# Two transformer blocks on one core: output gates computed inside the mLSTM heads, convolution taps run into the merge

## The chip, the cores and the metric

The kernel runs on one core of a Trainium2 chip. The metric is the device time of one execution in microseconds (us); the median of three runs of the kernel before is 3096.0 us (3094.24 to 3097.0). Five engines work beside each other: TensorE (PE) does the matrix products and transposes, VectorE (DVE), ScalarE (ACT) and GpSimd (POOL) the elementwise work, and SyncE (SP) issues the loads of weights.

## The reference, cut to what matters

Two depth-2 networks run one after the other over 256 tokens of width 1024 (the first has 256 context tokens beside them in its layer 0). The change touches only the first network's mixers: attention, a bidirectional mLSTM with four heads, and a convolution of 31 taps, merged by three sigmoid gates.

```python
def mlstm_readout(h, o_pre, norm_w, w_o):
    b, _, n, _ = h.shape
    hn = rmsnorm(h.transpose(0, 2, 1, 3), norm_w.reshape(MLSTM_HEADS, MLSTM_HEAD_DIM)).reshape(b, n, MLSTM_DIM)
    return (hn.astype(o_pre.dtype) * jax.nn.sigmoid(o_pre)) @ w_o

def conformer_conv(u, dw_w, dw_b, ln_w, ln_b, w_o):
    a, g = jnp.split(u, 2, axis=-1)
    h = dwconv(a * jax.nn.sigmoid(g), dw_w, dw_b)
    return jax.nn.silu(layernorm(h, ln_w, ln_b)) @ w_o
...
    def merge(conv_o, mlstm_o, attn_o, gate_pre):
        g_conv, g_mlstm, g_attn = jnp.split(jax.nn.sigmoid(gate_pre + branch_gate_b), N_BRANCH, axis=-1)
        return (g_conv * conv_o + g_mlstm * mlstm_o + g_attn * attn_o) @ w_out
```

## The kernel before, in words

Every large product is done in three passes (L414 to L416): weights and activations are split into a high and a low part, and high*high, high*low and low*high are added in PSUM. A chunk of eight 128x128 weight blocks is loaded by SP (L344), split by ACT and DVE into `wh` and `wl` (L323, L307), and taken in a fixed order from a stream (`_Stream.take`). `lin` multiplies one 128-wide strip of weights with all tokens: 24 products when the depth is eight blocks. Layer 0 of the first network works on 512 tokens (`nq` = 512), layer 1 on 256.

`mixers` (L784) goes through one layer's token mixers. First come the mLSTM's gate rows, the keys, values and queries of attention; then, by the list `ORDER` (L61), alternating heads ("m") and quarters of the convolution ("c"): m0 c0 m1 c1 m2 c2 m3 c3. A head (`mlstm`, L1136) computes q and k, the score tiles S (L1217) and the values V (L1171, the lines L435 to L437), and queues one follow-up per token segment (`mlstm_seg`, L1231; two segments in layer 0, one in layer 1). A follow-up is a chain: a row spread on PE (L1267), exponentials and products on DVE and ACT that make the weight tiles `mEh` and `mEl`, the products with V (L1309 to L1311), this twice (once for each direction), then the norm (POOL, L1251), four transposes (L1257) and a copy into `hs` (L1259). A quarter of the convolution (`glu_conv`, L1071) is two `lin`s and then 31 taps on DVE (L1097). After the last quarter come the output gates: eight `lin`s of `mlstm_gate` (L1195), whose tanh is multiplied into `hs` by a follow-up named "ogate".

Follow-ups lie in queues ("attn", "mlstm", "conv", "ogate") and are Python generators. Each `lin` credits all queues with its nominal time (`tick`, L393: 24 products of 512 columns count 5.12 us), and when the credit of a queue reaches its interval, one step of its generators is emitted. `flush` emits what is left. Steps marked `soon` get a higher priority, and a scheduler that runs when the kernel is built makes the final static order of each engine from priorities and simulated times. On the chip each engine follows that order and waits where a semaphore says so.

All tiles of the heads and of attention live in one memory pool, `head` (L795), which is closed after the flush of "mlstm", "ogate" and "attn" (L825). Then the pool `merge` is opened (L829) with the split inputs `bh` and `bl` and the sum `merged`. The merge takes attention's branch (`wba`), the convolution's (`wbc`, after `flush("conv")`) and the mLSTM's (`wbm`). For each 128 (layer 1: 256) output columns it does `po` (products with `bh` and `bl`, 4 or 8 blocks deep) and the gate's `pg` (products with the layer's own input, eight blocks deep), then tanh on ACT, a multiply on DVE and an add on POOL.

Of the kernel before, what the change touches and what calls it, by code (L numbers as in the profile page):

```python
# [24 lines left out]
AF = mybir.ActivationFunctionType  # L25
OP = mybir.AluOpType
# [5 lines left out]
KD = D // P  # L32
# [4 lines left out]
MH = 4  # L37
# [23 lines left out]
ORDER = [(kind, h) for h in range(MH) for kind in "mc"]  # L61
# [110 lines left out]
def _layout(inp):  # L172
# [11 lines left out]
    for l in range(DEPTH):  # L184
        w = a["w_in"][l]
# [7 lines left out]
        for kind, h in ORDER:  # L193
            if kind == "m":
                c = slice(h * 256, (h + 1) * 256)
                parts += [qkv[:, :1024][:, c], qkv[:, 1024:2048][:, c]]
            else:
                parts += [cu[:, h * P:(h + 1) * P], cu[:, 512 + h * P:512 + (h + 1) * P]]
        parts.append(mo)
# [15 lines left out]
        g = a["mlstm_gate_b"][l]  # L215
# [73 lines left out]
class _K:  # L289
# [494 lines left out]
    def mixers(self, l, st, xs, segs, nq):  # L784
# [5 lines left out]
        with ExitStack() as es:  # L790
# [4 lines left out]
            with tc.tile_pool(name=f"head{l}", bufs=1) as hp:  # L795
# [17 lines left out]
                for j in range(4):  # L813
                    for seg in segs:
                        self.queue("attn", (15.9 if l == 0 else 15) * slow, 2 if l == 0 else 1, self.attention(j, seg, seg * len(segs) // 2, kT, va, hp, ao))
                for kind, h in ORDER:
                    if kind == "m":
                        self.mlstm(l, h, st, xs, xq, segs, nq, rows, hp, hs)
                    else:
                        self.queue("conv", (6.4 if l == 0 else 8.7) * slow, 1,  # L820
                                   self.glu_conv(l, h, st, xq, segs, nq, mp, cv), early=False)
                self.queue("conv", (6.4 if l == 0 else 8.7) * slow, 1, self.conv_norm(l, nq, cv))
                for n in range(0, KD, G):
                    self.mlstm_gate(l, n, st, xq, nq, hs)
                for name in ("mlstm", "ogate", "attn"):  # L825
                    self.flush(name)
                if l == 0:
                    self.load_x()
            with tc.tile_pool(name=f"merge{l}", bufs=1) as gp:  # L829
                merged = gp.tile([P, KD, nq], F32, name="merged")  # L830
                for name, src, kt, b, first in (("wba", ao, 4, 2, True), ("wbc", cv, 4, 0, False),
                                                ("wbm", hs, 8, 1, False)):
# [303 lines left out]
    def mlstm(self, l, h, st, xs, xq, segs, nq, rows, hp, hs):  # L1136
# [26 lines left out]
        with self.soon():  # L1163
            S = [self.mlstm_scores(seg, i * 256, qT, kT, hp) for i, seg in enumerate(segs)]
        nc.gpsimd.tensor_copy(v[0][:, :, 256:258], self.onec[:, None, :].to_broadcast([P, 4, 2]))
# [13 lines left out]
        for i, seg in enumerate(segs):  # L1179
            self.queue("mlstm", (6.8 if l == 0 else 5.8), 2, self.mlstm_seg(h, seg, i * 256, nq, S[i], v, rows, hp, hs))  # L1180

# [13 lines left out]
    def mlstm_gate(self, l, n, st, xq, nq, hs):  # L1195

        G = 512 // nq
        bank = self.mmt()
        for i in range(G):
            self.lin(bank[:, i * nq:(i + 1) * nq], st["wi"], xq, KD)  # L1200
        t = self.tmp()
        with self.soon():
            self.act(t, bank, AF.Tanh, scale=0.5)
            for i in range(G):
                w = self.mnwh[l][:, n + i:n + i + 1]
                self.act(t[:, i * nq:(i + 1) * nq], t[:, i * nq:(i + 1) * nq], AF.Identity, scale=w, bias=w)

        def finish():
            if n // 2 == 3:
                self.flush("mlstm")  # L1210
            m = hs[:, n:n + G, :].rearrange("p g n -> p (g n)")
            self.tt(m, m, t, OP.mult)
            yield

        self.queue("ogate", (5.2 if l == 0 else 6.9), 1, finish())
# [15 lines left out]
    def mlstm_seg(self, h, seg, c0, nq, S, v, rows, hp, hs):  # L1231
# [27 lines left out]
        nc.scalar.copy(hs[:, 2 * h:2 * h + 2, c0:c0 + 256], pt.rearrange("p (e q) -> p e q", e=2))  # L1259
# [461 lines left out]
```

## Time and profile before

| what | value |
|---|---|
| median of three runs | 3096.0 us |
| profiled execution | 3097.4 us, of it a span of 3095.7 us |
| PE busy | 3047.0 us, 98% of the span, 21412 products |
| PE weight loads | 2745.8 us, 89% |
| DVE, ACT, POOL busy | 1866.6, 1468.1, 405.5 us |
| mean granted clock of TensorE | 0.994 |
| mixers and merge of layer 0 | about 44 to 690 us of the span |
| mixers and merge of layer 1 | about 1130 to 1548 us |

The profile gives, for each engine, when it was busy and what ended each wait. A matrix product shows as about 0.28 us (256 columns) because products overlap in the pipeline; what one costs is the distance from its start to the next one's. The granted clock is a share of 2.4 GHz, so 0.50 is 1.2 GHz. Times below are counted from the span's start.

### The profile page before, as it was taken

What the parts mean: (1) busy time and instruction counts of PE and PEld (TensorE: products, weight loads), DVE (VectorE), ACT (ScalarE), POOL (GpSimd) and SP (SyncE); (2) the same over time, 40 slices, a digit from 0 to 9 for tenths busy, and PEclk for the clock granted to TensorE, in tenths of its full rate; (3) what the DMA queues carried; (4) which work ended last, traced back from release to release, by engine and by line L of the source; (5) the groups of instructions that cost most, each with busy time, mean ns of one, the idle gap of its engine ahead of it and who ended that gap; (6) DMA issues with size and microseconds to landing.
All of it is one profiled execution on the core that took longest, in us unless ns stands there. A gap on an engine that the chain in (4) does not pass through costs nothing.

```text
span 3095.7 us, 52954 instructions
## 1 busy us (share of the span) xinstructions
PE 3047.0 (98%) x21412; PEld 2745.8 (89%) x21412; DVE 1866.6 (60%) x3064; ACT 1468.1 (47%) x2414; POOL 405.5 (13%) x419
## 2 busy tenths in 40 slices
PE   6999999999999999999999999999999999999999
PEld 4777878887777778899999999999999999999999
DVE  4467864336535546776587565576665665676664
ACT  4344463324323335455465444655544544654543
POOL 3212130112000033211100100122000000121000
PEclk9999999999999999999999999999999999999999
DMA  7423212324444423225555555444455554444553
GB/s 247 145 93 127 78 68 96 109 96 144 156 141 145 150 89 104 76 93 175 184 187 180 184 185 184 143 149 151 161 193 185 169 185 162 150 153 157 171 184 116
DMA packets 163429, 453.98 MB, mean 147 GB/s; under 512 B 14832, under 2 KB 66288, under 8 KB 162672
## 3 DMA queue, kind: packets, MB, share of 16 engines
q1 hardware_dynamic: 162464, 449.11, 43.9%
q8 instruction: 168, 2.75, 0.4%
q10 hardware_dynamic: 720, 1.49, 0.1%
q14 instruction: 77, 0.63, 0.1%
HBM read 447.13 MB, written 1.05 MB: 145 GB/s over the span
## 4 chain that ended last, share of the span: by engine, by line
PE 96%; DMA 1%; DVE 1%; ACT 1%; SPq 0%; issue 0%; POOL 0%; DVEq 0%; ACTq 0%; POOLq 0%
PE mm L414 25%; PE mm L416 25%; PE mm L415 25%; PE mm L436 2%; PE aux L605 2%; PE mm L437 2%; PE mm L435 2%; PE mm L428 1%; PE mm L429 1%; PE mm L427 1%; PE aux L1068 1%; DMA araw<-in_ada_dram 1%; PE aux L369 1%; PE aux L1569 1%; PE aux L1053 1%; PE aux L1043 1%
## 5 line engine op out<-in xcount | busy, mean ns | idle before, releaser
L307 DVE TENSOR_TENSOR wl<-raw,wh 128x1024 fp32r<-128x1024 f32 x746 | 922.2, 1239 | 780.9 <-ACT wh L323 763.0
L323 ACT CAST wh<-raw 128x1024 fp32r<-128x1024 f32 x746 | 782.5, 1051 | 1074.1 <-PE mm L415 736.4
L414 PE MATMUL mm<-xh,wh 128*128 128x256 f32 (+1 forms) x3680 | 1144.3, 311 | 4.2 <-ACT ao L301 3.0
L415 PE MATMUL mm<-xl,wh 128*128 128x256 f32 (+1 forms) x3680 | 1143.4, 311 | 0.0
L416 PE MATMUL mm<-xh,wl 128*128 128x256 f32 (+1 forms) x3680 | 1142.8, 311 | 0.0
L414 PEld LDWEIGHTS mm<-xh,wh 128*128 128x128 f32 x3680 | 699.3, 190 | 47.4 <-issue 8.4
L415 PEld LDWEIGHTS mm<-xl,wh 128*128 128x128 f32 x3680 | 699.5, 190 | 43.1 <-issue 9.6
L416 PEld LDWEIGHTS mm<-xh,wl 128*128 128x128 f32 x3680 | 699.3, 190 | 42.5 <-issue 7.5
L416 PE MATMUL mm<-ah,wl 128*128 128x256 f32 (+1 forms) x1056 | 317.5, 301 | 0.2 <-DVE wl L307 0.2
L415 PE MATMUL mm<-al,wh 128*128 128x256 f32 (+1 forms) x1056 | 317.6, 301 | 0.0
L414 PE MATMUL mm<-ah,wh 128*128 128x256 f32 (+1 forms) x1056 | 316.9, 301 | 0.0
L415 PEld LDWEIGHTS mm<-al,wh 128*128 128x128 f32 x1056 | 200.9, 190 | 9.1 <-issue 2.5
L416 PEld LDWEIGHTS mm<-ah,wl 128*128 128x128 f32 x1056 | 200.9, 190 | 9.1 <-issue 2.1
L414 PEld LDWEIGHTS mm<-ah,wh 128*128 128x128 f32 x1056 | 200.6, 190 | 8.7 <-issue 2.1
L310 POOL TENSOR_TENSOR small<-small,mhalf 128x2 f32<-128x2 f32 (+2 forms) x48 | 50.6, 1054 | 1051.7 <-DVE small L304 713.2
L310 POOL TENSOR_TENSOR ss<-ss,t 128x256 f32<-128x256 f32 (+1 forms) x68 | 72.1, 1061 | 623.7 <-ACT t L301 602.3
L304 DVE SCALAR_TENSOR_TENSOR cv<-glu,p,cv 128x512 f32<-128x512 f32 (+1 forms) x240 | 150.7, 628 | 3.5
L414 PE MATMUL mm<-bh,wh 128*128 128x512 f32 (+1 forms) x384 | 129.0, 337 | 1.3 <-ACT wh L323 0.7
L416 PE MATMUL mm<-bh,wl 128*128 128x512 f32 (+1 forms) x384 | 129.0, 337 | 0.3 <-DVE wl L307 0.3
L415 PE MATMUL mm<-bl,wh 128*128 128x512 f32 (+1 forms) x384 | 129.2, 337 | 0.0
L436 PE MATMUL mm<-wh,xl 128*128 128x256 f32 x448 | 127.8, 287 | 0.0
L437 PE MATMUL mm<-wl,xh 128*128 128x256 f32 x448 | 127.4, 286 | 0.0
(331 smaller groups left out, 4283.8 us busy)
## 6 DMA issues: line engine op xcount, KB each, us to landing
araw<-in_ada_dram SPq DMA_DIRECT2D x96, 512.0 KB, 3.9
raw<-in_a_wup_dram SPq DMA_DIRECT2D x88, 512.0 KB, 3.4
raw<-in_b_f1u_dram SPq DMA_DIRECT2D x88, 512.0 KB, 3.4
raw<-in_b_f2u_dram SPq DMA_DIRECT2D x88, 512.0 KB, 3.4
raw<-in_a_wi_dram SPq DMA_DIRECT2D x78, 512.0 KB, 3.3
raw<-in_b_wb_dram SPq DMA_DIRECT2D x72, 512.0 KB, 3.3
raw<-in_b_wi_dram SPq DMA_DIRECT2D x48, 512.0 KB, 3.4
raw<-in_a_wdn_dram SPq DMA_DIRECT2D x44, 512.0 KB, 3.3
```

Source lines behind the costliest of these rows:

```text
L304: self.nc.vector.scalar_tensor_tensor(out, in0, s, in1, op0=op0, op1=op1)
L307: self.nc.vector.tensor_tensor(out, in0, in1, op=op)
L310: self.nc.gpsimd.tensor_tensor(out, in0, in1, op=op)
L323: self.nc.scalar.copy(h, src)
L369: self.last_mm = self.nc.tensor.matmul(ps[0:32], x, x[:, 0:1].to_broadcast([P, 256]), start=True, stop=True).ins
L414: mm(ps, h, xh[:, k, cols], start=k == 0, stop=False)
L415: mm(ps, h, xl[:, k, cols], start=False, stop=False)
L416: self.last_mm = mm(ps, l, xh[:, k, cols], start=False, stop=k == kt - 1).ins
L435: mm(ps, xh, w[0], start=start, stop=False)
L436: mm(ps, xl, w[0], start=False, stop=False)
L437: mm(ps, xh, w[1], start=False, stop=stop)
L605: nc.tensor.matmul(ps[32 * j:32 * j + 32, c * 256:(c + 1) * 256], self.cpad[:, k, :], raw[:, j, :], start=k + c == 0, stop=k + c == KD)
```

## The change

The output gates move from the end of the heads into them: `mlstm_gate` runs for each head, before V in heads 0 to 2 and after V in head 3, and writes its tanh straight into `hs`. The follow-up's last step then multiplies the transposed result into `hs` (DVE) where it was copied before (ACT), and the queue "ogate" is gone. `ORDER` becomes one list for each layer: layer 0 is m0 c0 m1 c1 m2 m3 c2 c3, layer 1 stays m0 c0 m1 c1 m2 c2 m3 c3. Before c2 and c3 are computed, the "conv" queue is stepped until at most one earlier quarter is left. The intervals change: attention from 15.9 to 11.4 (layer 0) and from 9.0 to 7.5 (layer 1), the convolution from 6.4 to 8.0 (layer 0) and from 5.2 to 4.8 (layer 1). The merge takes the mLSTM's branch second and the convolution's last, so `flush("conv")` stands before the third branch.

```diff
@@ -58,7 +58,9 @@
 
 
 
-ORDER = [(kind, h) for h in range(MH) for kind in "mc"]
+
+ORDER = [[("m", 0), ("c", 0), ("m", 1), ("c", 1), ("m", 2), ("m", 3), ("c", 2), ("c", 3)],
+         [("m", 0), ("c", 0), ("m", 1), ("c", 1), ("m", 2), ("c", 2), ("m", 3), ("c", 3)]]
 
 STREAMS1 = {
     "wi": _chunks(WI_ORDER * KD),
@@ -190,13 +192,12 @@
         gates[:, 32:36], gates[:, 96:100] = mg[:, 8:12], mg[:, 12:16]
         rows = (np.arange(0, 512, 64)[:, None] + HALVES[None]).reshape(-1)
         parts = [gates, ak[:, rows[:P]], av, aq[:, rows][:, head]]
-        for kind, h in ORDER:
+        for kind, h in ORDER[l]:
             if kind == "m":
                 c = slice(h * 256, (h + 1) * 256)
-                parts += [qkv[:, :1024][:, c], qkv[:, 1024:2048][:, c]]
+                parts += [qkv[:, :1024][:, c], qkv[:, 1024:2048][:, c], mo[:, c]]
             else:
                 parts += [cu[:, h * P:(h + 1) * P], cu[:, 512 + h * P:512 + (h + 1) * P]]
-        parts.append(mo)
         s1["wi"].append(_pack(_fan(_blocks(np.concatenate(parts, axis=1)), 2), STREAMS1["wi"]))
         v = qkv[:, 2048:].reshape(2, KD // 2, P, MH, 256).transpose(3, 0, 2, 1, 4)
         s1["wv"].append(v.reshape(-1))
@@ -812,24 +813,25 @@
                     kT = self.key_parts(kT, hp)
                 for j in range(4):
                     for seg in segs:
-                        self.queue("attn", (15.9 if l == 0 else 15) * slow, 2 if l == 0 else 1, self.attention(j, seg, seg * len(segs) // 2, kT, va, hp, ao))
-                for kind, h in ORDER:
+                        self.queue("attn", (11.4 if l == 0 else 12.5) * slow, 2 if l == 0 else 1, self.attention(j, seg, seg * len(segs) // 2, kT, va, hp, ao))
+                conv = (8.0 if l == 0 else 8.0) * slow
+                for kind, h in ORDER[l]:
                     if kind == "m":
                         self.mlstm(l, h, st, xs, xq, segs, nq, rows, hp, hs)
                     else:
-                        self.queue("conv", (6.4 if l == 0 else 8.7) * slow, 1,
-                                   self.glu_conv(l, h, st, xq, segs, nq, mp, cv), early=False)
-                self.queue("conv", (6.4 if l == 0 else 8.7) * slow, 1, self.conv_norm(l, nq, cv))
-                for n in range(0, KD, G):
-                    self.mlstm_gate(l, n, st, xq, nq, hs)
-                for name in ("mlstm", "ogate", "attn"):
+                        if h > 1:
+                            while len(self.queues["conv"]["wait"] + self.queues["conv"]["live"]) > 1:
+                                self.step(self.queues["conv"])
+                        self.queue("conv", conv, 1, self.glu_conv(l, h, st, xq, segs, nq, mp, cv), early=False)
+                self.queue("conv", conv, 1, self.conv_norm(l, nq, cv))
+                for name in ("attn", "mlstm"):
                     self.flush(name)
                 if l == 0:
                     self.load_x()
             with tc.tile_pool(name=f"merge{l}", bufs=1) as gp:
                 merged = gp.tile([P, KD, nq], F32, name="merged")
-                for name, src, kt, b, first in (("wba", ao, 4, 2, True), ("wbc", cv, 4, 0, False),
-                                                ("wbm", hs, 8, 1, False)):
+                for name, src, kt, b, first in (("wba", ao, 4, 2, True), ("wbm", hs, 8, 1, False),
+                                                ("wbc", cv, 4, 0, False)):
                     if name == "wbc":
                         self.flush("conv")
                     bs = (gp.tile([P, KD, nq], F32R, name="bh"), gp.tile([P, KD, nq], F32R, name="bl"))
@@ -1162,6 +1164,8 @@
             self.step(self.queues["mlstm"])
         with self.soon():
             S = [self.mlstm_scores(seg, i * 256, qT, kT, hp) for i, seg in enumerate(segs)]
+        if h < MH - 1:
+            self.mlstm_gate(l, h, st, xq, nq, hs)
         nc.gpsimd.tensor_copy(v[0][:, :, 256:258], self.onec[:, None, :].to_broadcast([P, 4, 2]))
         pv = [self.mmt(), self.mmt()]
         for k in range(KD):
@@ -1178,6 +1182,8 @@
         self.tick(10.4)
         for i, seg in enumerate(segs):
             self.queue("mlstm", (6.8 if l == 0 else 5.8), 2, self.mlstm_seg(h, seg, i * 256, nq, S[i], v, rows, hp, hs))
+        if h == MH - 1:
+            self.mlstm_gate(l, h, st, xq, nq, hs)
 
     def pair(self, st, x, n):
 
@@ -1192,27 +1198,15 @@
             self.lin(q, st["wi"], x, KD)
             yield slice(i, i + 1), q[:, None, :]
 
-    def mlstm_gate(self, l, n, st, xq, nq, hs):
-
-        G = 512 // nq
-        bank = self.mmt()
-        for i in range(G):
-            self.lin(bank[:, i * nq:(i + 1) * nq], st["wi"], xq, KD)
-        t = self.tmp()
-        with self.soon():
-            self.act(t, bank, AF.Tanh, scale=0.5)
-            for i in range(G):
-                w = self.mnwh[l][:, n + i:n + i + 1]
-                self.act(t[:, i * nq:(i + 1) * nq], t[:, i * nq:(i + 1) * nq], AF.Identity, scale=w, bias=w)
-
-        def finish():
-            if n // 2 == 3:
-                self.flush("mlstm")
-            m = hs[:, n:n + G, :].rearrange("p g n -> p (g n)")
-            self.tt(m, m, t, OP.mult)
-            yield
-
-        self.queue("ogate", (5.2 if l == 0 else 6.9), 1, finish())
+    def mlstm_gate(self, l, h, st, xq, nq, hs):
+
+        for sl, ps in self.pair(st, xq, nq):
+            with self.soon():
+                t = hs[:, 2 * h:2 * h + 2, :][:, sl, :]
+                self.act(t, ps, AF.Tanh, scale=0.5)
+                for i in range(2)[sl]:
+                    w = self.mnwh[l][:, 2 * h + i:2 * h + i + 1]
+                    self.act(hs[:, 2 * h + i, :], hs[:, 2 * h + i, :], AF.Identity, scale=w, bias=w)
 
     def mlstm_scores(self, seg, c0, qT, kT, hp):
 
@@ -1256,7 +1250,8 @@
             for e in range(2):
                 nc.tensor.transpose(pt[:, e * 256 + qb * P:e * 256 + (qb + 1) * P], hh[:, qb, e * P:(e + 1) * P],
                                     self.ident)
-        nc.scalar.copy(hs[:, 2 * h:2 * h + 2, c0:c0 + 256], pt.rearrange("p (e q) -> p e q", e=2))
+        m = hs[:, 2 * h:2 * h + 2, c0:c0 + 256]
+        self.tt(m, m, pt.rearrange("p (e q) -> p e q", e=2), OP.mult)
 
     def mlstm_weights(self, d, h, seg, nsb, q0, S, rows, hp):
 
```

## Rows read from the trace of the kernel before

**Rows 1.** The page's part 1: busy us, share of the span, instructions.

```profile
PE 3047.0 (98%) x21412; PEld 2745.8 (89%) x21412; DVE 1866.6 (60%) x3064; ACT 1468.1 (47%) x2414; POOL 405.5 (13%) x419
```

**Rows 2.** Windows: length, then busy us (count) of PE, PEld, DVE, ACT, POOL; clock.

```profile
395.00:460.00 65.00, 60.88 (x298) 44.29 (x295) 41.30 (x93) 40.13 (x94) 17.54 (x15) 0.95 0.21 73
460.00:690.00 230.00, 229.48 (x1017) 189.53 (x1016) 86.53 (x102) 80.50 (x104) 26.81 (x20) 1.00 0.29 99
```

**Rows 3.** Waits of PE from 395 to 460 us: total, times, longest.

```profile
PE pv L1309 <- DVE mh L304: 0.6, 1, 0.6
PE aux L1053 <- ACT hs L1259: 0.5, 1, 0.5
PE mm L414 <- ACT bh L323: 0.3, 1, 0.3
```

**Rows 4.** Timeline of PE, layer 0, last head: start, us, operands [idle].

```profile
398.17 0.39 PE L1267 MATMUL aux<-msr,selr 100*128 100x256 f32 x1
400.08 0.83 PE L1267 MATMUL aux<-msr,selr 100*128 100x256 f32 x2 [1.52 <-DVE mE L304]
401.81 0.58 PE L1309 MATMUL pv<-mv,mEh 128*128 128x258 f32 x1 [0.90 <-ACT mEh L323]
...
404.71 0.63 PE L414 MATMUL mm<-xh,wh 128*128 128x512 f32 x1
```

**Rows 5.** Windows of the same columns around that stretch.

```profile
398.00:402.00 4.00, 1.58 (x5) 0.98 (x6) 3.48 (x11) 1.89 (x6) 1.17 (x1) 0.72 0.44 135
402.00:404.00 2.00, 1.77 (x7) 1.48 (x8) 2.00 (x8) 1.54 (x5) 0.15 (x2) 0.50 0.00 0
404.00:407.00 3.00, 3.00 (x12) 2.54 (x11) 3.00 (x8) 1.70 (x6) 0.80 (x1) 0.57 0.00 0
```

**Rows 6.** Timeline of ACT, layer 0, where the merge begins.

```profile
442.70 0.59 ACT L1259 COPY hs<-aux 128x512 f32<-128x512 f32 x1 [0.56 <-PE aux L1257]
...
457.61 0.37 ACT L1069 COPY ao<-aux 128x256 f32<-128x256 f32 x1 [6.52 <-PE aux L1068]
457.88 1.14 ACT L323 CAST bh<-ao 128x512 fp32r<-128x512 f32 x2
```

**Rows 7.** Timeline of PE at the same place.

```profile
458.90 0.40 PE L414 MATMUL mm<-xh,wh 128*128 128x512 f32 x1
```

**Rows 8.** Timeline of PE, layer 1: last V product, follow-up, transposes, merge.

```profile
1371.90 0.28 PE L437 MATMUL mm<-wl,xh 128*128 128x256 f32 x1
...
1374.42 0.28 PE L1309 MATMUL pv<-mv,mEh 128*128 128x258 f32 x1
...
1397.87 0.38 PE L1257 MATMUL aux<-cst,mh 128*128 128x128 f32 x2
...
1406.25 0.28 PE L414 MATMUL mm<-bh,wh 128*128 128x256 f32 x1
```

**Rows 9.** PE groups of 1372.1 to 1406.2 us, count and mean ns.

```profile
L414 PE MATMUL mm<-xh,wh 128*128 128x256 f32 x80 | 22.6, 283 | 0.0
...
L1311 PE MATMUL pv<-mv,mEl 128*128 128x258 f32 x14 | 4.0, 283 | 0.0
```

**Rows 10.** Timeline of ACT, layer 1, the same stretch.

```profile
1394.38 1.05 ACT L323 CAST wh<-raw 128x1024 fp32r<-128x1024 f32 x1 [1.48 <-PE mm L415]
...
1398.43 0.58 ACT L1259 COPY hs<-aux 128x512 f32<-128x512 f32 x1
1398.91 1.33 ACT L323 CAST bh<-ao 128x256 fp32r<-128x256 f32 x4
```

**Rows 11.** Waits of PE from 1370 to 1560 us.

```profile
PE mm L414 <- ACT t L301: 0.7, 1, 0.7
```

**Rows 12.** DVE groups of 370 to 398 us: the taps beside other work.

```profile
L304 DVE SCALAR_TENSOR_TENSOR cv<-glu,p,cv 128x512 f32<-128x512 f32 x22 | 16.9, 770 | 0.3
```

**Rows 13.** Timeline of POOL, layer 1: the norm of the last follow-up.

```profile
1392.65 3.42 POOL L1251 TENSOR_SCALAR mh<-mh,small 128x256 f32<-128x256 f32 x2
```

**Rows 14.** POOL groups of 44 to 460 us: the same norm in layer 0.

```profile
L1251 POOL TENSOR_SCALAR mh<-mh,small 128x256 f32<-128x256 f32 x16 | 17.6, 1108 | 0.8
```

## The prediction

> **What bounds the kernel now.** I read the page's first part, then the windows of the stretches that the change touches, then PE's waits and timelines there. PE is busy 98% of the span and every other engine at most 60% [rows 1], and its total work does not change: the same products are made in another order. So the change can only win what PE loses inside the two layers' mixers, and can only lose by opening new holes there. In the merge of layer 0 PE does 1017 products in 230 us without a hole, 0.226 us for one of 512 columns [rows 2]. In layer 1, from the last product for V at 1371.90 to the merge's first at 1406.25, there are 240 products of the output gates and of c3, 42 products of the follow-up and four transposes, that is 34.3 us over 286, or 0.120 us each for 256 columns [rows 8, 9]. These two prices carry the sum.
>
> **Where PE loses time today.** The end of layer 0's heads, 395 to 460 us, is the only such stretch in which PE's busy time falls visibly short and its clock is below full [rows 2]. A follow-up of head 3 stands there in PE's fixed order while DVE and ACT still make its weight tiles. From 398.17 to 404.71 PE waits 1.52 and 0.90 us [rows 4] and does some 13 small products, which at 0.12 us are 1.6 us of work: 4.9 us lost, part of it because the granted clock drops to 0.50, the lower of the two levels (1.2 GHz), in the middle of it [rows 5]. From 404 to 407 the mean clock is 0.57, so 0.43 x 3.0 = 1.3 us more go [rows 5]. Three later waits, on the follow-up and on `bh`, add 0.6 + 0.5 + 0.3 = 1.4 us [rows 3]. The sum is 7.6 us in layer 0. In layer 1 the tail costs one wait of 0.7 us, in the second branch of the merge, which today is the convolution's and waits for its tanh [rows 11].
>
> **Who ends last in front of the merge.** In layer 0 attention does: its last copy is at 457.61, after ACT sat idle 6.52 us, and the first `bh` split follows at 457.88, although the first `ao` rows had long been there [rows 6]. The mLSTM's last copy had been at 442.70 [rows 6]. In layer 1 the mLSTM's transposes end at 1398.2, its copy starts at 1398.43 and `bh` at 1398.91, while ACT had an idle 1.48 us at 1393 and attention had finished long before [rows 8, 10]. So I read: no tile of the pool `merge` is written before the last reader of the pool `head` is through.
>
> **The change part by part.**
>
> Gates inside the heads. No product is added. In layer 0, V of head 3 now has behind it the gate of head 3 (48 products), c2 and c3 (96): 144 x 0.226 = 32.6 us, where the gates alone had 43 us before. In layer 1 it has 96 x 0.120 = 11.5 us, where 28.7 us stood before. The weights move with the work in one stream, so SP's loads stay in order and number. Their tanh now holds a PSUM bank inside a head, for an ACT step that is `soon`; it frees a temporary tile. I take it at nothing; what hides it are the products for V that follow.
>
> Copy into a multiply. Twelve ACT copies of 0.59 us [rows 6, 10] go, twelve DVE multiplies in "ogate" go, and twelve that read PSUM come. DVE and ACT are not the bound; nothing. If that cover were gone, it would delay the bank's release by some 0.1 us each.
>
> Attention's interval. Eight units in layer 0, two at a time with four steps each, need 14 steps. At 15.9 that is 223 us of credit and the heads give 205, so the rest is flushed at the end; at 11.4 it is 160, and the credit at the end of V of head 3 is 175. Attention ends before, and the mLSTM becomes the last in front of the merge in both layers.
>
> The convolution late and in the merge. In layer 0 one quarter less is in the heads, two more in the merge: 62 taps of 0.77 us [rows 12] are 48 us of DVE in about 150 us of the first two branches. DVE is busy 86.5 of 230 us there today [rows 2]: room. Five steps a quarter and five for the norm, at 8.0, are 120 of credit, and c3 with two branches gives 154; in layer 1 it is 48 against 72. The convolution is thus ready before its branch, and layer 1's 0.7 us goes.
>
> Layer 0's tail, new. If the 7.6 us go, the merge starts at about 451. Behind V of head 3 lie 32.6 us of gates and quarters, and the follow-ups' own 60 products, 7.2 us: V ends at about 411. Today the chain takes 40.9 us from its first product at 401.81 to the copy at 442.70 [rows 4, 6], beside attention and taps, and starts 2.5 us after V where nothing else holds it [rows 8]. That gives 454.4 and `bh` half a us later. But `pg` of the merge needs no `bh`: at 458.90 PE does `pg` products while `bh` is being made [rows 7]. One `pg`, 24 x 0.226 = 5.4 us, covers up to 456. So the hole closes: -7.6 us, with bounds 0 (it reopens elsewhere) and -11 (shorter bubbles there go too, an estimate).
>
> Layer 1's tail, new. V of head 3 ends three gates later, 144 x 0.120 = 17.2 us, at 1389.2. Behind it lie 11.5 us, the follow-up's 42 products (5.0) and transposes (0.5): 17.0 us, and one `pg` of 48 products, 5.7: 22.7 us of cover. The chain took from 1372.0 to the first `bh` at 1398.91, 26.9 us, and a split more makes 27.4 [rows 8, 10]. As it is, a hole of 4.7 us; without the `pg`, 10.4. But in the chain of today work of the gates stands in PE's order ahead of both value products and transposes, and taps on DVE; I estimate some 4 us of it as order, not dependence. I take a hole of 1.5 us, nearer to the short end because nothing else is left to do for PE, with bounds 0 and 10.4.
> In that chain POOL's two norm multiplies take 3.42 us [rows 13], where sixteen in layer 0 take 1.11 each [rows 14]; taps run beside them. A rule of the Trainium skill bears on it: "SBUF — State Buffer", section on who interferes with whom, calls the port that DVE and GpSimd share an exclusive lock, which a DVE instruction with two SBUF inputs, as a tap is, and a POOL instruction take in turn. By it the multiplies would be 1.2 us shorter where no taps run: c3's taps start behind the head's gate then, and the hole would be 0.3 in place of 1.5, the sum -8.0. I leave it out of the sum, since c3's taps can still meet them; in the merge the same rule works against the change, where 62 taps come beside POOL's additions, but no product waits for those.
>
> **Sum.** -7.6 - 0.7 + 1.5 = -6.8 us. The profiled execution took 3097.4 us, 1.4 over the median, whose runs span 2.8; taken from the median it is 3089.
>
> **Rivals.**
> *The hole moves to layer 1.* For it: cover there falls from 34 to 17 us against a chain of 27, and `bh` waits for the pool. Against: `pg` can fill. Without filling, -8.3 + 10.4 = +2; with filling but the whole chain, -8.3 + 4.7 = -3.6. A hole of that length also halves the clock, as after the 1.5 us wait [rows 4, 5], for 1 to 2 us. 3093 to 3100, no change by measurement.
> By the Trainium skill, "TensorE: Matmul & The Clock Gate", section on how oscillation bites in real kernels, PE comes back at the lower clock after a long enough wait, so that each is paid twice. By that rule this rival ends at the upper of its two times; the trace agrees.
> *New order, new waits.* The static order comes from simulated times; a follow-up too early in it costs what rows 4 show, 5 to 7 us. One such place elsewhere cancels the gain: 3095.
> *Slower: the last head's chain is exposed in both layers.* In layer 0 m3 follows m2 directly, so its scores wait for head 2's follow-ups with 10.9 us (two `lin`s of c2) less in between. If that lag is kept to the end, chain and `bh` come 10.9 us later than above, at 466 against 456: +10 in place of -7.6, and with layer 1's +4.7, less 0.7, 3110; with half the lag 3104. It decides from the point where head 3's first follow-up product comes over 8 us after its V.
> *The change does not do what it says:* attention still ends last. Then as before, 3095.
>
> **How the numbers follow.** About 0.2% (6 us) is what a measurement of this kernel can tell from no change. Forecast, hole closed and layer 1 covered: 0.46, own range 3083 to 3090. Hole moved: 0.24. New waits, or attention still last: 0.15, together no change except 0.01. Slower: 0.15. So faster 0.47, same 0.38, slower 0.15. The range 3082 to 3102 takes in the bounds -11 and layer 1's open hole, and leaves out most of the slower case.
>
> **What would show it.** Right: PE's waits before the merge of layer 0 gone and its clock 1.00 there; `bh` directly after the last mLSTM transposes in both layers; attention's last copy over 10 us earlier than these; no wait in the third branch. Wrong: in layer 1 a wait of several us in front of the first `bh` product with a clock of 0.5 behind it; waits of row spreads (L1267) or value products in the middle of the heads; a wait at the third branch for `cv`.

## The result: 40 us slower, and where they arise

The changed kernel takes 3136.5 us (median, 3133.1 to 3141.2) against 3096.5 of the kernel before: ratio 1.0132, 95% interval 1.0114 to 1.0149. The prediction said 3089.0, with 3082 to 3102 as range. The sign was wrong, and the time lies far beyond the case that was priced as slower (3104 to 3110).

The page's part 1 of the changed kernel answers to [rows 1]; its span is 3136.4 us:

```profile
PE 3051.7 (97%) x21412; PEld 2754.4 (88%) x21412; DVE 1866.9 (60%) x3064; ACT 1460.0 (47%) x2402; POOL 402.4 (13%) x419
```

PE makes the same 21412 products, 4.7 us more busy in a span 40.7 us longer: the loss is waiting, and products at the lower clock. Where it lies is read from the first product with `bh`, which opens a layer's merge and has all the heads' products before it. In layer 0 it moved from 458.56 to 495.05, +36.5 us; in layer 1 from 1406.25 to 1449.96, so +7.2 more; behind that 3.0 us come back. The sum is 40.7. The first product with `bh` in layer 0 before; then, in the changed kernel, the same in layer 0, and in layer 1 with the two pairs of transposes ahead of it (the one of layer 1 before is in [rows 8]):

```profile
458.56 0.50 PE L414 MATMUL mm<-bh,wh 128*128 128x512 f32 x1 [0.32 <-ACT bh L323]
```

```profile
495.05 0.80 PE L415 MATMUL mm<-bh,wh 128*128 128x512 f32 x1 [0.78 <-ACT bh L324]
...
1447.58 0.68 PE L1251 MATMUL aux<-cst,mh 128*128 128x128 f32 x2 [4.52 <-POOL mh L1245]
1448.70 0.69 PE L1251 MATMUL aux<-cst,mh 128*128 128x128 f32 x2 [0.44 <-POOL mh L1245]
1449.96 0.58 PE L415 MATMUL mm<-bh,wh 128*128 128x256 f32 x1 [0.57 <-ACT bh L324]
```

The windows of the changed kernel at the end of layer 0's heads and of layer 1's (length, busy us and count of PE, PEld, DVE, ACT, POOL, clock, DMA share, GB/s), as [rows 2, 5]:

```profile
395.00:460.00 65.00, 51.27 (x275) 42.06 (x274) 49.27 (x101) 27.22 (x66) 9.93 (x8) 0.88 0.20 65
460.00:495.00 35.00, 16.70 (x62) 13.46 (x62) 27.74 (x55) 10.08 (x31) 8.31 (x8) 0.55 0.08 30
...
1442.80:1450.00 7.20, 1.66 (x8) 0.67 (x6) 6.58 (x13) 2.61 (x8) 2.79 (x3) 0.83 0.23 76
1450.00:1452.50 2.50, 2.50 (x12) 2.50 (x13) 2.50 (x8) 0.83 (x3) 0.00 (x0) 0.50 0.00 0
1452.50:1456.00 3.50, 3.50 (x24) 3.50 (x24) 3.25 (x8) 0.00 (x0) 0.00 (x0) 0.72 0.00 0
```

From 460 to 495 PE does 62 products in 35 us. Its largest waits from 340 to 500 us, and then all from 1380 to 1560 (total, times, longest), answer to [rows 3, 11]:

```profile
PE pv L1304 <- ACT mh L302: 11.0, 3, 5.3
PE aux L1251 <- POOL mh L1245: 6.1, 2, 4.3
PE pv L1304 <- ACT t L302: 6.0, 1, 6.0
PE pv L1304 <- DVE mh L305: 5.7, 1, 5.7
```

```profile
PE aux L1251 <- POOL mh L1245: 5.0, 2, 4.5
PE mm L415 <- ACT bh L324: 0.6, 1, 0.6
```

All but the last are links of the mLSTM's chain (value products `pv`, norm `mh`, transposes), and the last, on `bh`, follows from it. There is no other work left for PE: gates, c2 and c3 are done. So the last head's chain is exposed in both layers, as the third rival said. Its mechanism is another matter. The timeline of PE shows the lag far earlier, in head 1. Its last V product and its first row spread (L1262):

```profile
234.06 0.28 PE L438 MATMUL mm<-wl,xh 128*128 128x256 f32 x1
...
324.98 0.28 PE L1262 MATMUL aux<-msr,selr 100*128 100x256 f32 x1
```

91 us lie between them. In the kernel before it was 30:

```profile
217.70 0.28 PE L437 MATMUL mm<-wl,xh 128*128 128x256 f32 x1
...
247.76 0.28 PE L1267 MATMUL aux<-msr,selr 100*128 100x256 f32 x1
```

The products of those 91 us, by group, have ten attention scores (L1044) among them; the 30 us of the kernel before have four (its line is from the view of one tile, with durations and first and last start):

```profile
L1044 PE MATMUL aux<-akh,aq 128*128 128x512 f32 (+1 forms) x10 | 3.8, 378 | 0.0
```

```profile
L1042 PE MATMUL aux<-akh,aq x4: 279/333/397, 227.9 to 244.2; 128*128 128x256 f32 x2, 128*128 128x512 f32 x2
```

PE has no wait between 150 and 340 us in the changed kernel. So the lag itself costs nothing there: PE does other work meanwhile. It costs at the end, where the chain's late steps are all that is left.

### The profile page after: what moved, and what is told of

It reads as the page before. It is cut to its first block, busy times and chain, and to the rows that moved or that the text cites. A ratio compares the mean times of both kernels' runs of the same rounds, so it can differ in the third digit from the quotient of the medians.

```text
span 3136.4 us, 52953 instructions
## 1 busy us (share of the span) xinstructions
PE 3051.7 (97%) x21412; PEld 2754.4 (88%) x21412; DVE 1866.9 (60%) x3064; ACT 1460.0 (47%) x2402; POOL 402.4 (13%) x419
## 4 chain that ended last, share of the span: by engine, by line
PE 93%; DVE 3%; issue 1%; DMA 1%; ACT 1%; SPq 1%; POOL 0%; DVEq 0%; ACTq 0%; POOLq 0%
PE mm L415 25%; PE mm L417 25%; PE mm L416 25%; PE mm L436 2%; PE mm L437 2%; PE mm L438 2%; PE aux L606 2%; DVE cv L305 1%; PE mm L429 1%; PE mm L430 1%; PE mm L428 1%; PE aux L370 1%; PE aux L1070 1%; PE aux L1564 1%; PE aux L1055 1%
```

## Experiments: which part of the change does it

The theories: **A**, attention's faster release crowds out the mLSTM's chain; **B**, the gates inside the heads take its cover; **C**, m3 straight after m2 delays it. The table gives for every kernel its time and ratio, and, from PE's timeline in layer 0, how long after a head's last V product its first row spread comes (heads 0 to 3; below nothing where the spread comes first), with the number of attention scores between, and the start of the first product with `bh`. Each ratio is to the kernel before measured beside the variant (medians 3095.3 to 3096.5); a variant has two to ten executions.

| kernel | us | ratio [95%] | lag in us (scores), heads 0 to 3 | first `bh` |
|---|---|---|---|---|
| before | 3096 | 1 | 11 (2), 30 (4), 45 (2), 46 (4) | 458.6 |
| changed | 3136.5 | 1.0132 [1.0114, 1.0149] | 34 (4), 91 (10), 85 (8), 52 (2) | 495.1 |
| a1_attn_back | 3106.1 | 1.0032 [1.0020, 1.0045] | 12 (2), 17 (2), 23 (2), 23 (4) | 461.0 |
| a2_order_back | 3131.6 | 1.0113 [1.0083, 1.0142] | 34 (4), 91 (10), 90 (8), 62 (2) | 486.8 |
| b1_attn_fast | 3111.9 | 1.0059 [1.0036, 1.0082] | 31 (4), 86 (8), 90 (10), 57 (4) | 474.5 |
| b2_gates_in | 3137.8 | 1.0133 [1.0104, 1.0162] | 12 (2), 17 (2), 23 (2), 30 (4) | 477.8 |
| c1_cover_l1 | 3104.6 | 1.0025 [1.0016, 1.0035] | as a1 | 462.3 |
| c4_attn_mid | 3113.5 | 1.0055 [1.0038, 1.0072] | 16 (2), 39 (4), 51 (8), 34 (2) | 471.4 |
| d1_ada_late | 3116.3 | 1.0065 [1.0045, 1.0085] | 11 (2), 22 (4), 25 (2), -2 (0) | 434.7 |
| d2_bank_2_4 | 3200.3 | 1.0337 [1.0316, 1.0357] | 0 (0), 7 (1), 1 (0), -15 (0) | 455.0 |
| f1_before_ada_late | 3124.7 | 1.0087 [1.0072, 1.0102] | 5 (2), 13 (3), 10 (2), 32 (2) | 429.1 |
| f4_before_ada_attn | 3126.3 | 1.0094 [1.0079, 1.0109] | 21 (4), 48 (6), 60 (6), 56 (4) | 438.8 |
| f2_fast_attn_ada | 3139.7 | 1.0139 [1.0124, 1.0154] | 11 (2), 22 (4), 25 (2), -2 (0) | 432.3 |
| f3_slow_attn_ada | 3133.5 | 1.0116 [1.0099, 1.0133] | 2 (0), 4 (0), 7 (0), 7 (1) | 429.6 |
| g2_after_half | 3123.5 | 1.0091 [1.0076, 1.0106] | 34 (4), 65 (8), 59 (8), 28 (0) | 466.7 |
| g1_before_half | 3094.1 | 0.9995 [0.9986, 1.0004] | 11 (2), 18 (4), 25 (2), 41 (2) | 443.7 |
| g3_c1_half | 3088.8 | 0.9977 [0.9968, 0.9987] | 12 (2), 4 (0), 2 (0), -1 (0) | 432.8 |
| g4_before_half_attn | 3088.0 | 0.9974 [0.9965, 0.9984] | 11 (2), 29 (4), 42 (4), 45 (6) | 436.8 |
| h1_mlstm_sooner | 3141.7 | 1.0152 [1.0135, 1.0169] | 34 (4), 77 (10), 85 (9), 71 (2) | 494.7 |
| h2_g3_sooner | 3100.5 | 1.0017 [1.0008, 1.0026] | 12 (2), 10 (1), 4 (0), 10 (2) | 448.1 |

**a1_attn_back**, in the changed kernel:

```diff
-  self.queue("attn", (11.4 if l == 0 else 12.5) * slow, ...
+  self.queue("attn", (15.9 if l == 0 else 15) * slow, ...
```

> The changed kernel with one number put back: attention's interval 15.9 in layer 0 and 15 x slow in layer 1, as before. Theory A (attention's follow-ups, released faster, take the PSUM tiles and the engines' order from the mLSTM's, so that its chain lags through the heads): the lag goes, first row spread of head 1 within 50 us of its scores, time 3098 to 3110. Theory B (the gates inside the heads take the cover): 3132 to 3140. Theory C (m3 straight after m2): 3132 to 3140.

This one line takes back 30 of the 40 us. The last V product of head 1, its first spread, and the attention scores between them, in a1:

```profile
246.38 0.28 PE L438 MATMUL mm<-wl,xh 128*128 128x256 f32 x1
...
263.62 0.28 PE L1262 MATMUL aux<-msr,selr 100*128 100x256 f32 x1
```

```profile
L1044 PE MATMUL aux<-akh,aq 128*128 128x512 f32 x2 | 0.9, 444 | 0.0
```

Two scores in place of ten, 17 us in place of 91. In front of the merge a wait stays, PE's timeline of a1:

```profile
458.63 0.69 PE L1251 MATMUL aux<-cst,mh 128*128 128x128 f32 x2 [6.84 <-POOL mh L1245]
...
461.00 0.79 PE L415 MATMUL mm<-bh,wh 128*128 128x512 f32 x1 [0.79 <-ACT bh L324]
```

So the rest of the change, without the interval, costs 10 us by the medians. In the profiled executions it is 2.4 up to layer 0's merge and 7.6 from there to layer 1's, of which 2.4 come back behind it.

**a2_order_back**, in the changed kernel:

```diff
-ORDER = [[..., ("m", 2), ("m", 3), ("c", 2), ("c", 3)],
+ORDER = [[..., ("m", 2), ("c", 2), ("m", 3), ("c", 3)],
```

> The changed kernel with layer 0's order put back to m2 c2 m3 c3; all else stays. Theory C (m3 straight after m2 makes head 3's chain late): the hole in front of layer 0's merge goes, 3100 to 3115. Theory A (attention's interval) and theory B (gates inside the heads): the lag arises already in head 1, long before m3, so 3128 to 3140.

Heads 0 and 1 lag exactly as in the changed kernel, and the time falls by 5 us. C is a small part: that m3 follows m2 was the mechanism of the prediction's slower rival, and it is not what happened.

**b1_attn_fast**, the kernel before with the reverse of a1's edit. **b2_gates_in**, the kernel before with gates inside the heads alone:

```diff
-                for n in range(0, KD, G):
-                    self.mlstm_gate(l, n, st, xq, nq, hs)
-                for name in ("mlstm", "ogate", "attn"):
+                for name in ("mlstm", "attn"):
...
+        if h < MH - 1:
+            self.mlstm_gate(l, h, st, xq, nq, hs)
...
+        if h == MH - 1:
+            self.mlstm_gate(l, h, st, xq, nq, hs)
```

> The kernel before with attention's shorter interval alone (11.4 and 12.5 x slow). Theory A: the mLSTM's follow-ups lag here too, 3110 to 3130. Theories B and C: no loss, 3090 to 3098, since the gates still stand behind V of head 3 as cover.

> The kernel before with the output gates inside the heads alone (tanh into hs, the follow-up multiplies). Theory B: the cover behind V of head 3 is gone, 3115 to 3135, with PE waiting on the mLSTM in front of layer 0's merge. Theory A: the gates only move, 3096 to 3108, the most of it in layer 1, where 17 us of cover stand against a chain of 27. Theory C: 3094 to 3100.

b1 loses 15.9 us by the interval alone, with the lags of the changed kernel; the 43 us of gates behind V of head 3 hide the rest. b2 loses 41.7 without such lags, a little more than B expected: B holds as well. PE's waits in b2 say how, from 395 to 720 us and from 1380 to 1560:

```profile
PE aux L1246 <- POOL mh L1240: 7.2, 1, 7.2
PE pv L1299 <- ACT mh L300: 7.1, 2, 3.9
PE mm L413 <- ACT bh L322: 5.7, 2, 4.7
PE pv L1299 <- ACT t L300: 5.0, 1, 5.0
```

```profile
PE aux L1246 <- POOL mh L1240: 5.0, 2, 4.5
PE aux L489 <- POOL ss L309: 4.8, 1, 4.8
PE mm L413 <- ACT bh L322: 3.1, 2, 2.5
PE aux L498 <- POOL small L309: 1.1, 1, 1.1
```

The merge of layer 0 starts 19.2 us late, its second branch waits 4.7 for the convolution; layer 1 loses some 6.7 in front of its merge and 4.8 + 1.1 + 2.5 in its second branch: 39.0 of the 39.8 us by which the profiled executions differ. a1 has the gates inside too, and 31.7 us less: that is what the late convolution with its intervals, the merge's order and the attention flushed ahead of the mLSTM give back together once the gates are inside. They were not tried one by one.

## Experiments: by what attention holds up the chain

The small products of attention and of the mLSTM's chain go into tiles named `aux`, which share three PSUM banks. The queue `ada` accumulates two groups of modulation products for later stages in one of these banks, in the changed kernel from 41 to 154 and from 196 to 314 us. **A1**: the attention's tiles crowd the chain out of the two that are left. **A2**: it is the order of emission.

**c4_attn_mid** is c1 (below) with attention at 13.6 and 13.7:

> As the run with the interval put back and one quarter more behind V of head 3 in layer 1, but with attention's intervals half way (13.6 in layer 0, 13.7 x slow in layer 1). Theory A, read as a dose (the faster attention is released, the later the mLSTM's chain): the merge of layer 0 starts 15 to 20 us later than with 15.9, 3110 to 3125. Rival (a threshold: only where attention and the chain meet at the same tiles): either within 3 us of the run with 15.9, or as late as with 11.4, 3130.

The merge of layer 0 starts 9 us later than with 15.9, not 15 to 20 and not within 3: a dose, but a curved one. Of the 33 us in the start of the merge 24 lie between 13.6 and 11.4.

**d1_ada_late** and **d2_bank_2_4**, each in the changed kernel:

```diff
-                    self.queue("ada", 5.4, 1, ...
+                    self.queue("ada", 1e6, 1, ...
...
                 if l == 0:
                     self.load_x()
+                    self.queues["ada"].update(interval=5.4, credit=0.0)
```

```diff
-    ... k.banks(3, 3) as k.psum:
+    ... k.banks(2, 4) as k.psum:
```

> The changed kernel with the queue ada (modulation products of later stages, which holds one of the three aux banks of PSUM all through layer 0's heads) held back to the merge. Theory A1 (attention crowds the mLSTM out of the aux banks, of which only two are free): with a third one the first row spread of head 1 comes within 50 us of the end of its V, where it came 91 us after it, and the merge of layer 0 starts 20 to 35 us earlier: 3100 to 3118. Theory A2 (it is the order of emission and priority, banks don't matter): the merge starts within 5 us of the changed kernel's 495, 3128 to 3140.

> The changed kernel with PSUM shared out as 2 banks for the large products and 4 for aux, in place of 3 and 3. The time itself will be worse, since two banks leave the large products no third one to run into while the two are read; it is not the question. Theory A1 (aux banks): first row spread of head 1 within 50 us of the end of its V. Theory A2 (order): 80 to 95 us after it, as in the changed kernel.

Both bear A1 out. With one aux bank more and attention still at 11.4 the lag of head 1 falls from 91 us to 22 in d1 and to 7 in d2; d2's last V product of head 1 and the first spread:

```profile
271.85 0.28 PE L438 MATMUL mm<-wl,xh 128*128 128x256 f32 x1
...
279.18 0.36 PE L1262 MATMUL aux<-msr,selr 100*128 100x256 f32 x1
```

V of head 1 ends 38 us later in d2 than in the changed kernel, which leaves the chain more time, but the spread comes 46 us earlier (279.2 against 325.0). The one group of waits that PE has left from 150 to 460 us in d2:

```profile
PE mm L415 <- ACT glu L302: 3.3, 1, 3.3
```

The mLSTM's waits are gone from there. What d2 loses is behind it: from the first `bh` to the end it takes 102 us more than the changed kernel. About half of that are waits of the large products for one of their two banks, from 460 to 1750 us:

```profile
PE mm L415 <- ACT t L302: 49.7, 35, 2.1
```

d1 brings the merge's start forward by 60 us, of which some 18 are ada's own products (248 of them now come later, at 71 ns), so 42 where 20 to 35 were expected, and the time by 20.

**f1, f4, f2, f3** move all of ada into the merge at an interval of 4.2 (d1's edit with 4.2): f1 the kernel before; f4 the same with attention at 11.4 in layer 0; f2 the changed kernel with attention at 15 x slow in layer 1 and c1's order; f3 that with 15.9 in layer 0.

> The kernel before with the queue ada alone held back to the merge (there at an interval of 4.2). Theory A1 (a third free aux bank matters as soon as attention and the mLSTM's chain are both in work): the 7.6 us lost at the end of layer 0's heads shrink, 3086 to 3093. Rival (with attention at 15.9 two banks are enough): 3094 to 3100, the ada products only change places.

> The kernel before with ada held back and attention at 11.4 in layer 0. Attention at 11.4 (and 12.5 in layer 1) alone cost 15.9 us there. Theory A1: that loss was the aux bank, and with it free the gates as cover and an early attention are both there, 3082 to 3094. Rival A2 (order of emission): 3105 to 3113.

> The changed kernel (attention 11.4 in layer 0) with ada held back to the merge at an interval of 4.2, and in layer 1 attention at 15 x slow and the order m2 m3 c2 c3. Against 3116 with ada alone held back: the 12 us in which PE waited for ada's loads at the end of the merge go, and 2 to 3 in layer 1: 3098 to 3104. What is left over the kernel before is the last head's chain, open in both layers (11 and 4 us).

> As the run before, but with attention at 15.9 in layer 0. Theory A1: with a third bank the interval no longer matters much, so within 5 us of it, 3096 to 3106. Rival A2 (the interval itself makes the order): better than it by 10 us or more.

All four times lie above what was expected, by 13 to 36 us even over the nearest of the ranges, because the moved loads hold up PE and its clock falls with it (the granted clock from 460 to 720 us is 0.94 in f1, 1.00 in the kernel before). The waits for the loads from 460 to 720 us in f1, and in d1 (from 420) at its interval of 5.4:

```profile
PE aux L605 <- DMA araw<-in_ada_dram: 24.7, 7, 4.6
```

```profile
PE aux L606 <- DMA araw<-in_ada_dram: 10.0, 3, 3.7
```

I had taken the move as free. The heads, which end before these loads, can still be compared: f2 and f3 start the merge 2.7 us apart, where the same two intervals with ada in the heads are 33 apart. So up to layer 0's merge the interval matters in the changed kernel only while a bank is missing. (Their times are 6.2 us apart, a little over the 5 that A1 allowed; 2.4 of it arise between the two merges.) In the kernel before (f4, f1) 9.7 us stay of 16, and heads 1 and 2 of f4 still lag 48 and 60 us with all three banks free: there A1 is not the whole, and no run shows the rest.

**g2, g1, g3, g4** move only ada's second group, at an interval that spreads its loads:

```diff
-  self.queue("ada", 5.4, 1, self.ada_group(0, 1, ada), self.ada_group(0, 2, ada))
+  self.queue("ada", 5.4, 1, self.ada_group(0, 1, ada))
+  self.ada2 = self.ada_group(0, 2, ada)
...
                 if l == 0:
                     self.load_x()
+                    self.queue("ada", 9.0, 1, self.ada2)
```

g2 is the changed kernel, g1 the kernel before, g3 is c1, g4 is g1 with attention at 14.0 in layer 0.

> The changed kernel with ada's second group alone moved from layer 0's heads into its merge, at an interval of 9.0. Theory A1 (aux bank): first row spread of head 1 within 50 us of the end of its V (91 in the changed kernel), merge of layer 0 at 440 to 460, of which 8.5 us are the moved products, and 3100 to 3112. Rival A2 (order of emission): merge near 485, 3130 to 3138. If ada's loads stall PE in the merge again, its waits there are over 5 us and the start of the merge decides.

> The kernel before with ada's second group alone moved into the merge, at 9.0. Theory A1: the bank is short here too, if less, and the hole of 7.6 us in front of the merge shrinks by half or more: 3086 to 3093. Rival (two banks are enough at 15.9): 3094 to 3099.

> The changed kernel with attention's interval put back, layer 1's order m2 m3 c2 c3, and ada's second group moved into the merge at 9.0. Without the move it took 3104.6. Theory A1: 3094 to 3101, within 8 us of the same with fast attention. What is left over the kernel before is the open chain of the last head in both layers, 4 us in layer 1 and 8 to 10 in layer 0. Rival A2: 3103 to 3107.

> The kernel before with ada's second group moved into the merge and attention at 14.0 in layer 0, so that attention ends before the last head's chain. Theory A1: all of the hole in front of layer 0's merge goes, with the gates as cover behind V of head 3: 3084 to 3091, the version that beats both. Rival A2: 3096 to 3106, between the kernel before and the one with attention at 11.4 (3111.9).

No wait for ada's loads is left in the merge. g3 and g4 beat the kernel before, by 7 and 8 us (g3 by more than expected); in g3 this is what remains of the waits on the norm, from 340 to 720 and from 1340 to 1560 us:

```profile
PE aux L1253 <- POOL mh L1247: 2.0, 2, 1.2
```

```profile
PE aux L1253 <- POOL mh L1247: 2.9, 2, 1.9
```

g1 can't be told from the kernel before: freeing the bank alone is not enough. g4 gains with attention let go faster as well; the same interval with ada left in place wasn't run, so how much of the gain needs the bank is open. g2 misses: 13 us better, not 25 or more. Its head 0 lags 34 us as in the changed kernel, although ada's first group is through at 154, before V of head 0 ends (157), and heads 1 and 2 still lag 65 and 59 with three banks free. A1 as a bank that is missing at that moment doesn't explain this. A backlog of attention, built up while the first group held its bank, would look so, but no run shows it.

**h1_mlstm_sooner** (changed kernel) and **h2_g3_sooner** (g3):

```diff
-  self.queue("mlstm", (6.8 if l == 0 else 5.8), 2, ...
+  self.queue("mlstm", (4.5 if l == 0 else 5.8), 2, ...      (h1)
+  self.queue("mlstm", (5.2 if l == 0 else 4.4), 2, ...      (h2)
```

> The changed kernel with the mLSTM's own interval in layer 0 at 4.5 in place of 6.8; attention and ada stay as fast and as placed as they are there. Theory A2 (a step waits for the attention tiles that were emitted ahead of it): fewer than 6 attention score products between the end of V of head 1 and its first row spread (10 in the changed kernel), the spread within 60 us, the merge of layer 0 15 to 35 us earlier, 3100 to 3120. Rival (attention's load as such, done by 420 us, takes the engines and banks whatever the order): 3130 to 3140.

> The changed kernel with attention's interval put back, layer 1's order m2 m3 c2 c3 and ada's second group in the merge at 9.0 (3088.8 us), and the mLSTM's intervals from 6.8 and 5.8 to 5.2 and 4.4. If the holes left there (3 us before layer 0's merge, 4 in layer 1's) are late emission: 3082 to 3087. If they are the chain itself, V, weights, products, norm, transposes one behind the other: 3087 to 3091.

Against A2: the mLSTM's own interval doesn't take the chain past attention. Ten scores still lie ahead of head 1's first spread in h1, which is at 310:

```profile
310.10 0.28 PE L1262 MATMUL aux<-msr,selr 100*128 100x256 f32 x1
```

A2 could mean another order than this interval sets, which wasn't tried. h2 misses both expectations, because it makes layer 0 worse. PE waits for the norm there, from 340 to 500 us,

```profile
PE aux L1253 <- POOL mh L1247: 10.8, 1, 10.8
```

and attention's last products stand behind that wait in PE's order. So attention is now last, by ACT's timeline,

```profile
447.15 0.37 ACT L1073 COPY ao<-aux 128x256 f32<-128x256 f32 x1 [2.25 <-PE aux L1072]
447.42 2.18 ACT L324 CAST bh<-ao 128x512 fp32r<-128x512 f32 x4
```

and `bh` comes 15 us later than in g3. From there to layer 1's merge it is 5.3 us better (961.8 against 967.1). The interval 4.4 in layer 1 alone, on g3, wasn't run.

## Experiment: the hole in layer 1

**c1_cover_l1**: a1 with, in layer 1, the order m2 m3 c2 c3.

```diff
-         [..., ("m", 2), ("c", 2), ("m", 3), ("c", 3)]]
+         [..., ("m", 2), ("m", 3), ("c", 2), ("c", 3)]]
```

> The changed kernel with attention's interval put back, and in layer 1 the order m2 m3 c2 c3, so that one quarter more (48 products of 0.12 us, 5.8 us) lies behind V of head 3. Theory D (the 6.9 us that PE loses in front of layer 1's merge are nothing but missing cover for the last head's chain): the hole shrinks to 1 to 2 us, 3099 to 3102. Rival (m3 straight after m2 delays the chain by as much): 3104 to 3109.

In layer 1 of a1 it takes 23.7 us from the last V product to the first `bh`, for 142 products that at the prediction's 0.120 us are 17.0 us of work: a hole of 6.7 (the expectation put it at 6.9). In c1 it takes 26.9 us for 190 products, 22.8 us of work: a hole of 4.1, between the two expectations. The time, 3104.6, lies in the rival's range and can't be told from a1's 3106.1. The waits from 1380 to 1560 us in c1:

```profile
PE aux L1251 <- POOL mh L1245: 2.9, 2, 1.9
...
PE mm L415 <- ACT bh L324: 0.6, 1, 0.6
```

So 5.8 us of cover bought 2.6: from V's end to the first `bh` it now takes 3.2 us longer (1387.2 to 1414.1, in a1 1392.5 to 1416.3). That PE's covering products stand in the chain's way would explain this; no run shows it apart.

## Why the prediction was wrong, step by step

**Attention's interval** is the step that failed. Its credit was worked out rightly: attention ends at 419.7 in place of 458.0 and the mLSTM becomes the last. ACT's last copy for attention in the changed kernel (before: [rows 6]):

```profile
419.37 0.37 ACT L1071 COPY ao<-aux 128x256 f32<-128x256 f32 x1 [0.47 <-PE aux L1070]
```

But the price of releasing it faster was put at nothing. It is 30 of the 40 us (a1), 15.9 alone in the kernel before (b1). Attention and the chain share the aux banks, and of these one was held by ada for long stretches; in the changed kernel a bank more takes most or all of the lag away (d1, d2), though what is left of it in g2 stays open. The trace of before would have shown both, as PE products into `aux`.

**Layer 0's tail** rested on a chain that starts 2.5 us after V "where nothing else holds it", a row of layer 1 [rows 8]. In layer 0 of the kernel before head 3's V ended at 352.3 and its first spread came at 398.2 [rows 4]: 46 us, and 45 in head 2. That lag could have been read:

```profile
352.30 0.28 PE L437 MATMUL mm<-wl,xh 128*128 128x256 f32 x1
```

The -7.6 came out as +2.4 even with the interval put back. With a bank free as well the heads' end has no such hole (g3). The rival *Slower* named the outcome, a last chain exposed in both layers, but not its cause: putting its order m2 m3 back saves 5 us (a2). Its sign, "over 8 us after its V", says little, since the spread comes 52 us after V in the changed kernel and came 46 after it before. Its price had a slip too: a hole of 10 us behind a gain of 7.6 is +2.4, not +10, so by its own terms 3102, not 3110. That the time came out slower is no credit to it.

**Gates inside the heads** were "at nothing". Alone they cost 41.7 us (b2), since they leave the place behind V of head 3 where they were cover. With the rest of the change around them 10 us are left (a1), most of it in front of layer 1's merge.

**Layer 1's tail** was mis-sized: +1.5 foretold, 6.7 measured, in the changed kernel as in a1 and b2, which have the gates inside and the old order there. The chain was as estimated: 27.4 less some 4 us of order make 23.4, measured are 23.7 (V's end 1426.3 to `bh` 1449.96). The wrong term is the `pg` that would fill: the first product of the merge in PE's order is the one with `bh`, in both layers and kernels, and no `pg` precedes it. Without it the same sum gives 23.4 - 17.0 = 6.4.

The rival *The hole moves to layer 1* was right on this hole and on the clock behind it, though not on the time. After waits of 4.52, 0.44 and 0.57 us PE came back at the lower clock: the mean is 0.50 in the 2.5 us from 1450.0 on and 0.72 in the next 3.5 (the last two rows of the windows above). That is 0.50 x 2.5 + 0.28 x 3.5 = 2.2 us lost behind `bh`, beside 5.5 us of waits in front of it. The section on oscillation of the Trainium skill's page "TensorE: Matmul & The Clock Gate" says that PE starts again at the lower clock after a long enough wait, and the trace agrees with these 2.2 us.

**The convolution in the merge** was right: no wait stands at the third branch, layer 1's 0.7 us [rows 11] is gone.

## What to carry to other kernels

Where two chains draw tiles from the same few PSUM banks, releasing one faster may not be free: count in the trace how many of its tiles lie between the other's ready point and its first step, before and after. An accumulation that holds a bank of that ring for a hundred microseconds is a first thing to move, and its loads need room where it goes. And how late a follow-up starts is read from the same layer, not from the one where nothing is in its way.

## What the runs showed of the hardware

The norm's two multiplies on POOL in layer 1, 3.42 us before [rows 13], take 2.06 in the changed kernel, with six taps on DVE from 1446.16 on. In layer 0 of the changed kernel the last two take 1.83 with DVE idle. The three lines (POOL, DVE, POOL):

```profile
1446.59 2.06 POOL L1245 TENSOR_SCALAR mh<-mh,small 128x256 f32<-128x256 f32 x2
```

```profile
1446.16 3.35 DVE L305 SCALAR_TENSOR_TENSOR cv<-glu,p,cv 128x256 f32<-128x256 f32 x6
```

```profile
490.45 1.83 POOL L1245 TENSOR_SCALAR mh<-mh,small 128x256 f32<-128x256 f32 x2
```

The prediction weighed "SBUF — State Buffer" of the Trainium skill, on who interferes with whom, and expected 1.2 us less where no taps run. 1.4 us less came with taps running. So the forecast came true for another reason than the one it gave: beside these taps the pair is only 0.2 us longer than with DVE idle. What ran on DVE in the middle of the pair before, and not in the changed kernel, is the split of a weight chunk, an operation with two inputs in SBUF as well:

```profile
1392.99 1.22 DVE L307 TENSOR_TENSOR wl<-raw,wh 128x1024 fp32r<-128x1024 f32 x1
```

The first of the two multiplies, which this split overlaps, takes 2.29 us before and 0.93 in the changed kernel; the second takes 1.15 in both. That fits this rule of the Trainium skill with the split in the place of the taps. It is read from overlap in time; no run moved the split alone.
